# Up-projections of a two-layer encoder: three couples of column groups per layer, and a finished group's convolution work issued after the next group's first weight splits

## The chip, the cores and the metric

The kernel runs on one core of one Trainium2 chip. The time is device microseconds of one execution. The kernel before takes 2450.95 us, the median of three runs (2449.8 to 2451.17). The profile is of one further execution, which took 2449.38 us; its profiled span is 2447.3 us, so 2.08 us of that time lie around the span.

Engines are named as in the profile: PE is TensorE (matmuls), PEld its weight loads, DVE is VectorE, ACT is ScalarE, POOL is GpSimd, SP is SyncE. SP and POOL here mostly issue transfers.

## The reference, cut to what matters

Two layers, 256 positions, width 2048, everything in float32. Each layer has a token mixer (a gated MLP with a spatial gate, then a latent attention) and after it the sub-layer that the change touches, a gated MLP with a causal depthwise convolution of width 3 between the up-projection and the activation:

```python
D_MODEL = 2048
SEQ = 256
D_FF = 5504
CONV_W = 3

def conv_ffn(x, w_up, conv_w, conv_b, w_down):
    h = x @ w_up                                   # 256 x 2048 by 2048 x 11008
    h = lax.conv_general_dilated(h, conv_w[:, None, :], window_strides=(1,),
                                 padding=[(CONV_W - 1, 0)],
                                 dimension_numbers=('NWC', 'WIO', 'NWC'),
                                 feature_group_count=C) + conv_b
    a, g = jnp.split(h, 2, axis=-1)
    return (jax.nn.silu(g) * a) @ w_down
```

Around it stand a residual sum and a layer norm: `x = layer_norm(ALPHA * x + f, g, b)`.

## The kernel before, in words

**Exactness by splitting.** A float32 weight tile `raw` is split on the chip into two halves in a faster matmul format: ACT casts it to `wh` (line 134) and DVE subtracts to get `wl` (line 137). Activations are split the same way and kept as `xhl`. A product is then the sum of three: high by high, low by high, high by low.

**The up-projection's groups.** The 11008 columns of `w_up` are worked in 22 groups (0 to 21) of 512 columns; a group's weights come as four chunks of 1 MB, each one SP transfer into one of three `raw` buffers. `feed.next()` hands out the next chunk and first issues the loads and splits of the two chunks behind it. A group is worked in one of two ways.

- A *plain* group (`plain`, `prod_a`) has columns on the partitions: the weights are the stationary operand and `xhl` streams past. Per chunk 16 matmuls of 512 streamed columns (`wh`) and 16 of 256 (`wl`), so 128 matmuls per group into four of the eight PSUM banks.
- A *couple* of groups (`summed`) has tokens on the partitions: the weights stream past stationary pieces of `xhl`. Its eight chunks are taken in the order `UP_PAIRS`. Four of them go through `eight` (24 matmuls of 512 columns), the four in `UP_SEVEN` through `seven`, a seven-product scheme for a 2x2 block product (21 matmuls of 512). It needs sums of activations (`sums`, made once per layer by `combine_up`, tiles `xu`) and sums of weights (`ts`, line 144, and their split halves `th`, `tl`), and all eight banks, named q3, p2, e, q4, p1, q5, p7, p6. Afterwards DVE folds the banks together (`rest`, lines 475 to 478, and four final sums), and PE turns the four results back to columns on the partitions with 16 transposes of 128x128 (`turn_back`, line 1049), which stand after the first chunk of the following plain group.

**After a group.** `pair` makes one 128-row tile of the activation from two accumulators: ACT copies half a bank (`lo`, line 409), DVE adds the other half (`h`, line 411), then the convolution takes one ACT pass (line 1023) and two DVE passes (lines 1024, 1026), then SiLU on ACT (line 1040) and a product on DVE (line 1041). A plain group has two pairs; they run while the next group is on PE. The two `h` reads of a pair are what frees a bank for the next owner. After a couple there are four pairs, called by the plain group behind it (`both`), without the `lo` and `h` steps.

**Small work among the groups.** The table `EARLY` places, by group and chunk, the four `combine_up`, the residual's last scaling (`restore`, four DVE operations of 128x512 each and two row loads on the SP queue, lines 738 to 742) and the copying of the residual's two halves to memory (`park`, POOL queue, line 718). From group 10 on, `jobs` copies eight chunks of the down-projection's weights, split and summed in advance, out to memory (`park_all`: loads `praw`, casts `pwh`, `pth`, line 172, subtractions line 173, sums line 161, four stores per chunk, lines 166 and 189, all on the POOL queue); the calls are counted out by group and chunk.

**What sets the order.** The program's text gives priorities, and a scheduler orders each engine's queue from it with its own model of durations; what is marked `keep_in_program_order` stays as written. Every engine works its queue strictly in order. On-chip memory is handed out from pools: 14 tiles of 8 KB per partition in "big" (weight halves, `xhl`, the residual, most of the activation), 6 in "side", 3 `raw`.

Of the kernel before, what the change touches and what calls it, by code (L numbers as in the profile page):

```python
# [15 lines left out]
P = 128  # L16
# [53 lines left out]
LEAD = 5  # L70
KEEP = {"wide": 4, "seven": 6, "parked": 6}

UP = [(1,), (2,), (3,), (4,), (5, 6), (7,), (8, 9), *((i,) for i in range(10, 22))]
UP_PAIRS = [0, 2, 1, 3, 5, 4, 6, 7]
UP_SEVEN = (2, 3, 4, 6)
EARLY = {(1, 2): ("restore", 0), (2, 1): ("combine", 0), (2, 2): ("restore", 1), (2, 3): ("park", 0),
         (3, 1): ("restore", 2), (3, 2): ("combine", 1), (3, 3): ("restore", 3), (4, 0): ("park", 1),
         (4, 1): ("combine", 2), (4, 2): ("combine", 3)}


def plan(n_k):
# [140 lines left out]
def trunk(ctx: ExitStack, tc: tile.TileContext, x, xT, gm_in, gm_wout, ffn_up, ffn_dn,  # L222
# [807 lines left out]
    def ffn(layer, ln, acc, end, last):  # L1030
# [39 lines left out]
        def combine_up(p):  # L1070

            x = xhl[p // 2][:, p % 2 * 2 : p % 2 * 2 + 2]
            y = tp.tile([P, 2, S], F32, tag="t2", name=f"upy{layer}_{p}", bufs=T2)
            nc.vector.tensor_tensor(y, x[:, :, 0:S].bitcast(F32), x[:, :, S : 2 * S].bitcast(F32), ALU.add)
            if len(sums) % 2 == 0:
                rooms.append(slot([P, 2, 8 * P], f"xu{layer}_{p}", F32R))
            sums[p] = combine(f"u{layer}_{p}", rooms[-1][:, len(sums) % 2, :], y[:, 0], y[:, 1])

        early = {"restore": old.restore, "park": old.park, "combine": lambda i: combine_up(UP_SEVEN[i])}

        def plain(gi, turned):

            nt, nk = (4, 4) if gi < 21 else (2, 8)
            acc = [bank(f"up{layer}_{gi}_{f}") for f in range(nt)]
            for c in range(KD // nk):
                hi, lo = feed.next()
                prod_a(acc, xhl, range(nk * c, nk * c + nk), hi, lo)
                if c == 0 and turned:
                    for i, t in enumerate(turned[2]):
                        turn_back(turned[1][i % 2], t, i // 2)  # L1090
                if turned and 0 < c < 3:
                    both(turned[0][c - 1], turned[1][c - 1])
                if (gi > 9 and c > 0) or (gi, c) == (7, 3):
                    next(jobs, None)
                if (gi, c) in FIRST:
                    acts.make(*plan(NF_FF)[0][FIRST.index((gi, c))])
                if gi == 1 and c == 0:
                    after(1, 1, None)
                    both(0, hb)
                if (gi, c) in EARLY:  # L1100
                    name, i = EARLY[gi, c]
                    early[name](i)
            for f in range(nt // 2):
                pair(2 * gi + f, acc[f], acc[nt // 2 + f])

        def summed(gis):

            acc = Banks(f"up{layer}_{gis[0]}", DIRECT + OWN)
            for p in UP_PAIRS:
                a = [[x_parts(xhl, 2 * p + j, b) for j in range(2)] for b in range(2)]  # L1110
                got = feed.next()
                if p in UP_SEVEN:
                    acc.seven(a, sums[p], *got, turned=512, across=True)
                    if p == UP_SEVEN[-1]:
                        rest = acc.rest()
                else:
                    acc.eight(a, *got, across=True)
            for n, t in zip(DIRECT, rest):
                nc.vector.tensor_tensor(t, acc.acc[n], t, ALU.add)
            return gis, [[bank(f"upr{layer}_{gi}_{f}") for f in range(2)] for gi in gis], rest  # L1120
# [440 lines left out]
```

## Time and profile before

| what | value |
|---|---|
| median of three runs | 2450.95 us (2449.8 to 2451.17) |
| the profiled execution | 2449.38 us, span 2447.3 us |
| PE busy | 2440.4 us, 100% of the span |
| DVE busy | 2191.0 us, 90% |
| ACT busy | 1512.4 us, 62% |
| POOL busy | 140.6 us, 6% |
| granted TensorE clock | 1.00 |
| mean memory traffic | 256 GB/s |

The busy share of PE says that it is never long without work; how fast that work goes is read from the starts of its matmuls, since their ends are modelled. The up-projection's plain groups and couples follow each other on PE without other work between them: in layer 0 groups 1 to 4, then the couple of 5 and 6, group 7, the couple of 8 and 9, and groups 10 to 21. Layer 1 repeats this about 955 us later.

### The profile page before, as it was taken

To read this page: it belongs to the slowest core of one execution; us is meant where nothing else is said; L and a number is where in the kernel's file an instruction comes from. 1 tells how busy PE (TensorE), PEld (TensorE's weight loads), DVE (VectorE), ACT (ScalarE), POOL (GpSimd) and SP (SyncE) were. 2 spreads that over 40 slices of the span, in tenths; PEclk is the share of its full clock that TensorE was granted. 3 is DMA by queue.
4 is the path that set the end of the run, shared out by engine and by line. 5 is a ranking of instruction groups with operands and counts; after the bars stand their busy time and mean duration, and the time that the engine had idled before them with its cause. 6 is when DMAs were issued, how large, how long until landed. Compare 5 with 4: busy or idle time off the path is not lost.

```text
span 2447.3 us, 32249 instructions
## 1 busy us (share of the span) xinstructions
PE 2440.4 (100%) x12151; PEld 2065.3 (84%) x12151; DVE 2191.0 (90%) x2914; ACT 1512.4 (62%) x1997; POOL 140.6 (6%) x261
## 2 busy tenths in 40 slices
PE   9999999999999999999999999999999999999999
PEld 7888888888888888888888888988888888888887
DVE  7999999899998889998889897878798999888998
ACT  6666665566576655666665566665655666666553
POOL 0000000001010000011000000000000001010000
PEclk9999999999999999999999999999999999999999
DMA  7555666658796755799988885533575589898894
GB/s 293 203 205 205 233 202 205 207 173 304 254 296 241 239 205 194 258 359 374 341 318 320 320 298 172 188 141 126 207 272 184 181 323 375 321 371 300 314 353 178
DMA packets 128763, 627.37 MB, mean 256 GB/s; under 512 B 11592, under 2 KB 15184, under 8 KB 91616
## 3 DMA queue, kind: packets, MB, share of 16 engines
q1 hardware_dynamic: 94224, 462.47, 53.5%
q0 software_dynamic: 34384, 162.86, 17.9%
q8 instruction: 95, 1.56, 0.3%
q14 instruction: 60, 0.49, 0.1%
HBM read 552.35 MB, written 72.93 MB: 256 GB/s over the span
## 4 chain that ended last, share of the span: by engine, by line
PE 97%; DVE 1%; DMA 1%; ACT 0%; issue 0%; POOL 0%; ACTq 0%; DVEq 0%; POOLq 0%
PE up L242 30%; PE ub L242 16%; PE dn_q L242 8%; PE dn_p L242 6%; PE v_q L242 5%; PE v_p L242 4%; PE up_q L242 3%; PE up_p L242 3%; PE wo_q L242 2%; PE dn_e L242 2%; PE wo_p L242 2%; PE upf L242 2%; PE mo L242 2%; PE v_e L242 2%; PE mkv L242 1%; PE qn L242 1%
## 5 line engine op out<-in xcount | busy, mean ns | idle before, releaser
L137 DVE TENSOR_TENSOR wl<-raw,wh 128x1024 fp32r<-128x1024 f32 (+5 forms) x611 | 936.3, 1550 | 108.9 <-ACT wh L134 77.4
L134 ACT CAST wh<-raw 128x1024 fp32r<-128x1024 f32 (+5 forms) x611 | 790.9, 1318 | 307.2 <-PE up L242 67.8
L242 PE MATMUL up<-xhl,wh 128*128 128x512 f32 x2112 | 492.9, 390 | 0.0
L242 PEld LDWEIGHTS up<-xhl,wh 128*128 128x128 f32 x2112 | 392.3, 188 | 78.7
L134 ACT CAST th<-ts 128x1536 fp32r<-128x1536 f32 x196 | 203.7, 1051 | 173.9 <-DVE ts L144 144.2
L242 PEld LDWEIGHTS up<-xhl,wl 128*128 128x128 f32 x2112 | 262.4, 192 | 5.1
L242 PE MATMUL up<-xhl,wl 128*128 128x256 f32 x2112 | 265.1, 283 | 0.0
L137 DVE TENSOR_TENSOR tl<-ts,th 128x1536 fp32r<-128x1536 f32 x196 | 231.6, 1219 | 7.9 <-ACT th L134 3.3
L242 PE MATMUL ub<-wh,xhl 128*128 128x512 f32 x552 | 172.0, 393 | 0.0
L144 DVE TENSOR_TENSOR ts<-ts,raw 128x512 f32<-128x512 f32 x196 | 134.7, 687 | 2.0
L242 PEld LDWEIGHTS ub<-wh,xhl 128*128 128x128 f32 x552 | 103.6, 188 | 23.2 <-issue 1.9
L144 DVE TENSOR_TENSOR ts<-raw 128x1024 f32<-128x1024 f32 x98 | 119.5, 1219 | 2.2 <-DMA raw<-in_gm_in_dram 0.8
L242 PE MATMUL ub<-wl,xhl 128*128 128x512 f32 x276 | 107.5, 389 | 0.0
L242 PE MATMUL v_q<-wh,xhl 128*128 128x512 f32 x224 | 70.8, 391 | 0.0
L242 PEld LDWEIGHTS ub<-wl,xhl 128*128 128x128 f32 x276 | 51.8, 188 | 10.9
L242 PE MATMUL v_p<-wh,xhl 128*128 128x512 f32 x192 | 59.9, 389 | 0.0
L242 PEld LDWEIGHTS v_q<-wh,xhl 128*128 128x128 f32 x224 | 42.1, 188 | 9.7 <-ACT wh L134 0.9
L832 ACT ACTIVATE lny<-lnt,lncol 128x128 f32<-128x128 f32 x96 | 36.6, 471 | 15.7 <-PE lnt L828 15.6
L161 DVE TENSOR_TENSOR praw<-praw 128x512 f32<-128x512 f32 x64 | 43.9, 686 | 0.5
L242 PE MATMUL v_q<-wl,xhl 128*128 128x512 f32 x112 | 43.6, 389 | 0.0
L242 PE MATMUL mo<-wh,oT 128*128 128x512 f32 x128 | 42.7, 411 | 0.0
L242 PEld LDWEIGHTS v_p<-wh,xhl 128*128 128x128 f32 x192 | 36.0, 188 | 7.5
(2073 smaller groups left out, 4824.9 us busy)
## 6 DMA issues: line engine op xcount, KB each, us to landing
raw<-in_ffn_up_dram SPq DMA_DIRECT2D x172, 1024.0 KB, 5.9
raw<-in_gm_in_dram SPq DMA_DIRECT2D x93, 1024.0 KB, 5.3
raw<-in_ffn_dn_dram SPq DMA_DIRECT2D x68, 1024.0 KB, 7.7
raw<-in_gm_wout_dram SPq DMA_DIRECT2D x48, 1024.0 KB, 6.4
praw<-in_ffn_dn_dram POOLq DMA_DIRECT2D x16, 1024.0 KB, 12.5
keptth<-pth POOLq DMA_DIRECT2D x16, 1024.0 KB, 8.5
kepttl<-ptl POOLq DMA_DIRECT2D x16, 1024.0 KB, 8.7
fth<-keptth POOLq DMA_DIRECT2D x16, 1024.0 KB, 9.5
```

The source lines that it names most:

```text
L134: cast = self.nc.scalar.copy(hi, raw)
L137: self.nc.vector.tensor_tensor(lo, raw, hi.bitcast(F32), ALU.subtract)
L144: add = lambda o, a, b: self.nc.vector.tensor_tensor(o, a, b, ALU.add)
L161: add = lambda o, a, b: pin(nc.vector.tensor_tensor(o, a, b, ALU.add))
L242: recent[0] = nc.tensor.matmul(o, l, r, start=start, stop=stop, skip_group_check=True)
L832: nc.scalar.activation(y[:, j], t[:, j * P : (j + 1) * P], AF.Identity, bias=lncol[:, o : o + 1], scale=lncol[:, g : g + 1])
```

## The change

The table `UP` of a layer goes from two couples, (5, 6) and (8, 9), to three, (3, 4), (6, 7) and (9, 10). So groups 3, 4 and 10 are no longer plain, groups 5 and 8 are, and from group 1 on 15 groups are plain where 17 were (the last, group 21, is half a group).

With it: the four `combine_up` move into groups 1 and 2, since the first couple needs them there; the activation sums go to the "side" pool; the second half of the residual is scaled and copied out late (written at groups 12, 16 and 17); the calls of `jobs` begin one group later and come four to a group, not three, in groups 13 to 15. And a plain group no longer calls `pair` at its end: it puts its two pairs on a list, and the next group's first chunk calls them (`settle`) after `feed.next()`, that is, after the splits which that call issues. From group 19 on the list is emptied at the group's end as before.

```diff
-UP = [(1,), (2,), (3,), (4,), (5, 6), (7,), (8, 9), *((i,) for i in range(10, 22))]
+UP = [(1,), (2,), (3, 4), (5,), (6, 7), (8,), (9, 10), *((i,) for i in range(11, 22))]
-EARLY = {(1, 2): ("restore", 0), (2, 1): ("combine", 0), (2, 2): ("restore", 1), (2, 3): ("park", 0),
-         (3, 1): ("restore", 2), (3, 2): ("combine", 1), (3, 3): ("restore", 3), (4, 0): ("park", 1),
-         (4, 1): ("combine", 2), (4, 2): ("combine", 3)}
+EARLY = {(1, 1): ("restore", 0), (1, 2): ("combine", 0), (1, 3): ("combine", 1), (2, 0): ("restore", 1),
+         (2, 1): ("combine", 2), (2, 2): ("park", 0), (2, 3): ("combine", 3),
+         (12, 0): ("restore", 2), (16, 0): ("restore", 3), (17, 0): ("park", 1)}
...
-                rooms.append(slot([P, 2, 8 * P], f"xu{layer}_{p}", F32R))
+                rooms.append(slot([P, 2, 8 * P], f"xu{layer}_{p}", F32R, "side"))
...
+        waiting = []
+
+        def settle():
+
+            while waiting:
+                pair(*waiting.pop(0))
...
                 hi, lo = feed.next()
+                settle()
                 prod_a(acc, xhl, range(nk * c, nk * c + nk), hi, lo)
...
-                if (gi > 9 and c > 0) or (gi, c) == (7, 3):
+                if (gi > 10 and (c > 0 or 12 < gi < 16)) or (gi, c) == (8, 3):
                     next(jobs, None)
...
-            for f in range(nt // 2):
-                pair(2 * gi + f, acc[f], acc[nt // 2 + f])
+            waiting.extend((2 * gi + f, acc[f], acc[nt // 2 + f]) for f in range(nt // 2))
+            if gi > 18:
+                settle()
...
                 got = feed.next()
+                settle()
                 if p in UP_SEVEN:
```

The change as the scheduler lays it out, at three places. **PE, second chunk of the first couple of layer 0.** The names are banks and weight halves; `wh165` and `wh157` are the couple's second chunk, `wh166` and `wh158` its third. Before, with the couple of 5 and 6:

```order
L242 MATMUL up0_5_p1_7092<-wh165_7002,xhl1_1_5899 128x512 x2
L242 MATMUL up0_5_p1_7092<-wl165_7003,xhl1_1_5899 128x512
L242 MATMUL up0_5_q4_7091<-th165_7004,xhl1_1_5899 128x512 x2
L242 MATMUL up0_5_q4_7091<-tl165_7005,xhl1_1_5899 128x512
L242 MATMUL up0_5_q5_7093<-th165_7004,xu0_2_6495 128x512 x2
L242 MATMUL up0_5_q5_7093<-tl165_7005,xu0_2_6495 128x512
L242 MATMUL up0_5_p7_7094<-th165_7004,xu0_2_6495 128x512 x2
L242 MATMUL up0_5_p7_7094<-tl165_7005,xu0_2_6495 128x512
L242 MATMUL up0_5_p6_7095<-th165_7004,xu0_2_6495 128x512 x2
L242 MATMUL up0_5_p6_7095<-tl165_7005,xu0_2_6495 128x512
```

Now, with the couple of 3 and 4, the last products of the second chunk stand behind most of the third:

```order
L242 MATMUL up0_3_q4_6630<-wh158_6635,xhl1_0_5898 128x512 x2
L242 MATMUL up0_3_q4_6630<-wl158_6636,xhl1_0_5898 128x512
L242 MATMUL up0_3_p7_6633<-th157_6573,xu0_2_6333 128x512 x2
L242 MATMUL up0_3_p7_6633<-tl157_6574,xu0_2_6333 128x512
L242 MATMUL up0_3_q4_6630<-wh158_6635,xhl1_0_5898 128x512 x2
L242 MATMUL up0_3_q4_6630<-wl158_6636,xhl1_0_5898 128x512
L242 MATMUL up0_3_q3_6627<-wh159_6704,xu0_2_6333 128x512 x2
L242 MATMUL up0_3_q3_6627<-wl159_6705,xu0_2_6333 128x512
L242 MATMUL up0_3_p2_6628<-wh159_6704,xhl1_1_5899 128x512 x2
L242 MATMUL up0_3_p6_6634<-th157_6573,xu0_2_6333 128x512 x2
L242 MATMUL up0_3_p6_6634<-tl157_6574,xu0_2_6333 128x512
```

Counted in the couple's matmuls, p7 was first written after 39 of them and is now after 60, p6 after 42 and now after 71; p1 stays at 30, and q5 goes from 36 to 39. In the couples of 6 and 7 and of 9 and 10 p7 comes after 58 and 42, p6 after 65 and 61; before, in the couple of 8 and 9, after 48 and 59.

**DVE at the start of that couple.** `h` rows read the last plain group's banks and free them; `wl` of the couple's third chunk is `wl166` before and `wl158` now. Before:

```order
L411 TENSOR_TENSOR h_0a8_7052<-up0_4_0_6858,lo_0a8_7050 128x256
L1024 SCALAR_TENSOR_TENSOR c_0a8_7054<-h_0a8_7052,cst_176,c_0a8_7054 128x255
L411 TENSOR_TENSOR h_0g8_7060<-up0_4_2_6860,lo_0g8_7058 128x256
L1026 SCALAR_TENSOR_TENSOR c_0a8_7054<-h_0a8_7052,cst_176,c_0a8_7054 128x254
L1024 SCALAR_TENSOR_TENSOR c_0g8_7062<-h_0g8_7060,cst_176,c_0g8_7062 128x255
L1026 SCALAR_TENSOR_TENSOR c_0g8_7062<-h_0g8_7060,cst_176,c_0g8_7062 128x254
L1041 TENSOR_TENSOR act0_1_7049<-s0_8_7066,c_0a8_7054 128x256
L411 TENSOR_TENSOR h_0a9_7071<-up0_4_1_6859,lo_0a9_7069 128x256
L137 TENSOR_TENSOR wl166_7097<-raw166_6958,wh166_7096 128x2048
L1024 SCALAR_TENSOR_TENSOR c_0a9_7073<-h_0a9_7071,cst_176,c_0a9_7073 128x255
L411 TENSOR_TENSOR h_0g9_7079<-up0_4_3_6861,lo_0g9_7077 128x256
```

Now:

```order
L137 TENSOR_TENSOR wl158_6636<-raw158_6534,wh158_6635 128x2048
L316 TENSOR_TENSOR xsu0_6_6620<-xsu0_6_6620,upy0_6_6618 128x128
L411 TENSOR_TENSOR h_0a4_6643<-up0_2_0_6390,lo_0a4_6641 128x256
L317 TENSOR_TENSOR xsu0_6_6620<-upy0_6_6618,xsu0_6_6620 128x128
L144 TENSOR_TENSOR ts159_6703<-raw159_6584 128x1024
L326 TENSOR_TENSOR xu0_4_6522<-xsu0_6_6620,xu0_4_6522 128x512
L1024 SCALAR_TENSOR_TENSOR c_0a4_6645<-h_0a4_6643,cst_176,c_0a4_6645 128x255
L411 TENSOR_TENSOR h_0g4_6651<-up0_2_2_6392,lo_0g4_6649 128x256
L1026 SCALAR_TENSOR_TENSOR c_0a4_6645<-h_0a4_6643,cst_176,c_0a4_6645 128x254
L144 TENSOR_TENSOR ts159_6703<-ts159_6703,raw159_6584 128x512
L1024 SCALAR_TENSOR_TENSOR c_0g4_6653<-h_0g4_6651,cst_176,c_0g4_6653 128x255
L137 TENSOR_TENSOR wl159_6705<-raw159_6584,wh159_6704 128x1536
```

The third chunk's `wl` went from behind three of the four bank reads to ahead of all of them, and the fourth chunk's sums and split stand among them. The two remaining bank reads, `h_0a5` and `h_0g5`, follow 4 and 7 rows after the last row shown, with `ts159`, `act0_0` and the first piece of `tl159` between.

**SP, where the second half of the residual's rows are loaded.** Before, among the loads of groups 3 and 4:

```order
L738 DMA lnp0_20_6715<-in_ln_rows_dram 128x512
L738 DMA lnp0_21_6717<-in_ln_rows_dram 128x512
L109 DMA raw158_6509<-in_ffn_up_dram 128x2048
L109 DMA raw159_6557<-in_ffn_up_dram 128x2048
L109 DMA raw160_6641<-in_ffn_up_dram 128x2048
L738 DMA lnp0_30_6812<-in_ln_rows_dram 128x512
L738 DMA lnp0_31_6814<-in_ln_rows_dram 128x512
```

Now, among the loads of group 12 (chunks 192 to 195):

```order
L738 DMA lnp0_20_8397<-in_ln_rows_dram 128x512
L109 DMA raw192_8079<-in_ffn_up_dram 128x2048
L738 DMA lnp0_21_8399<-in_ln_rows_dram 128x512
L738 DMA lnp0_30_9294<-in_ln_rows_dram 128x512
L109 DMA raw193_8135<-in_ffn_up_dram 128x2048
L738 DMA lnp0_31_9296<-in_ln_rows_dram 128x512
L109 DMA raw194_8205<-in_ffn_up_dram 128x2048
```

All four row loads moved behind the last couple; the scheduler did not leave those of the fourth quarter at group 16, where the text has them. The POOL queue's copy of the residual's second half (line 718) moved with them, from ahead of the first `praw` to behind the third.

## The prediction

> **What bounds the kernel now.** I read the page first, then the chain of waits in order of time, then the stages one by one, then the waits and the timelines inside a couple.
>
> ```profile
> span 2447.3 us, 32249 instructions
> PE 2440.4 (100%) x12151; PEld 2065.3 (84%) x12151; DVE 2191.0 (90%) x2914; ACT 1512.4 (62%) x1997; POOL 140.6 (6%) x261
> PE 97%; DVE 1%; DMA 1%; ACT 0%; issue 0%; POOL 0%; ACTq 0%; DVEq 0%; POOLq 0%
> ```
>
> PE is the bound: 97% of the chain is its own. A change gains what it takes out of PE's stream and loses what it makes PE wait for. VectorE at 90% comes next. The chain through layer 0's up-projection (start, length, matmuls; the last row from the whole span's chain):
>
> ```profile
> 816.36 83.36 PE up L242 x480
> 899.72 1.36 PE up_q L242 x6
> 940.52 5.54 PE up L242 x32
> 946.06 1.75 PE upr L1049 x16
> 964.49 1.36 PE up_q L242 x6
> 1005.64 5.54 PE up L242 x32
> 1012.93 250.06 PE up L242 x1440
> ```
>
> The plain lengths count to the next row's start, so they are rates and not modelled ends. A plain group of 128 matmuls takes 83.36 / 480 x 128 = 22.23 us, and 250.06 / 1440 gives the same: the plain groups run without a gap. The first couple lasts from 899.72 to 940.52, 40.80 us for 180 matmuls, 226.7 ns each; its 16 transposes take 1.75 us in the next group. The second lasts 1005.64 - 964.49 = 41.15 us, 0.35 more for the same work. What was late there, and how near VectorE is, say the waits of this stretch and the stages (length, PE, weight loads, VectorE, ScalarE, POOL; clock, DMA share, GB/s):
>
> ```profile
> PEld up_q L242 <- DVE tl L137: 0.4, 1, 0.4
> PEld up_p L242 <- DVE h_0a L411: 0.2, 1, 0.2
> 899.72:940.52 40.80, 40.80 (x181) 33.78 (x181) 37.04 (x43) 25.38 (x28) 0.00 (x0) 1.00 0.53 185
> 940.52:964.49 23.97, 23.97 (x145) 21.43 (x145) 22.41 (x36) 14.13 (x21) 0.00 (x0) 1.00 0.59 195
> 964.49:1005.64 41.15, 41.15 (x181) 33.61 (x181) 38.82 (x44) 24.70 (x27) 0.00 (x0) 1.00 0.55 191
> 1096.30:1140.80 44.50, 44.50 (x257) 39.39 (x257) 40.39 (x56) 28.56 (x40) 5.19 (x9) 1.00 1.00 387
> ```
>
> A couple leaves VectorE 2 to 4 us. There PE already waits for it, for a split and for a bank read, if only by tenths.
>
> **The change, part by part.** *A couple for two plain groups.* Two plain groups cost 2 x 22.23 = 44.46 us, a couple 40.80 + 1.75 = 42.55: 1.91 us less in each layer, **3.82 us** in both. This is PE's own stream, so the gain is in the end time unless a wait eats it.
>
> *VectorE in a couple.* Prices from the first couple's timeline, where it works without a break. What counts is the step to the next start, a little less than the printed length (second column); the last two rows are of group 3:
>
> ```profile
> 905.69 2.29 DVE L137 TENSOR_TENSOR wl<-raw,wh 128x2048 fp32r<-128x2048 f32 x1 [1.31 <-ACT wh L134]
> 907.90 0.48 DVE L1024 SCALAR_TENSOR_TENSOR c_0a<-h_0a,cst,c_0a 128x255 f32<-128x255 f32 x1
> 908.29 0.42 DVE L411 TENSOR_TENSOR h_0g<-up,lo_0g 128x256 f32<-128x256 f32 x1
> 908.63 0.47 DVE L1026 SCALAR_TENSOR_TENSOR c_0a<-h_0a,cst,c_0a 128x254 f32<-128x254 f32 x1
> 909.02 1.22 DVE L144 TENSOR_TENSOR ts<-raw 128x1024 f32<-128x1024 f32 x1
> 910.15 0.48 DVE L1024 SCALAR_TENSOR_TENSOR c_0g<-h_0g,cst,c_0g 128x255 f32<-128x255 f32 x1
> 910.55 0.68 DVE L144 TENSOR_TENSOR ts<-ts,raw 128x512 f32<-128x512 f32 x1
> 911.15 0.47 DVE L1026 SCALAR_TENSOR_TENSOR c_0g<-h_0g,cst,c_0g 128x254 f32<-128x254 f32 x1
> 911.54 1.75 DVE L137 TENSOR_TENSOR wl<-raw,wh 128x1536 fp32r<-128x1536 f32 x1
> 913.21 0.68 DVE L144 TENSOR_TENSOR ts<-ts,raw 128x512 f32<-128x512 f32 x1
> 913.82 0.42 DVE L1041 TENSOR_TENSOR act<-s,c_0a 128x256 f32<-128x256 f32 x1
> ...
> 859.10 0.28 DVE L314 TENSOR_TENSOR xsu<-upy 128x128 f32<-128x128 f32 x1
> 859.30 0.28 DVE L315 TENSOR_TENSOR xsu<-upy 128x128 f32<-128x128 f32 x1
> ```
>
> So 2.21 us for 2048 columns, 1.67 for 1536, 1.13 for 1024, 0.60 for 512, 0.20 for 128; 0.39 for a convolution pass, 0.34 for an `h` or an activation product. An eight-product chunk takes 2.21, a seven-product one 1.13 + 3 x 0.60 + 2 x 1.67 = 6.27, a pair 2 x (0.34 + 2 x 0.39) + 0.34 = 2.58. A couple asks 4 x (2.21 + 6.27) + 2 x 2.58 = 39.1 of its 40.80 us. The Trainium skill speaks against a third couple here: VectorE: DVE Perf Modes, "The DRAIN you can't avoid", has the next operation start only when the pipeline has emptied. By printed lengths the same work comes to about 42.7 us and every couple would lose 1.9; the steps above disagree, and so do the first couple's 40.80 us.
>
> *The first couple comes two groups earlier.* From group 1's start to the third chunk's `wl` of that couple VectorE now has six plain chunks (6 x 2.26 = 13.6), the two pairs of group 0 (3.8), two `restore` (8 x 0.60 = 4.8), group 1's pairs (5.2), most of four `combine_up` at 2 x 0.60 + 4 x 0.20 (7) and the couple's first two chunks (8.5): 43 us. In groups 1 and 2 before, it stood still for 4.4 and 1.1 us:
>
> ```profile
> 811.10:833.30 22.20, 22.20 (x131) 19.74 (x130) 17.84 (x26) 14.16 (x19) 0.00 (x0) 1.00 0.73 258
> 833.30:855.50 22.20, 22.20 (x129) 19.66 (x128) 21.15 (x36) 12.48 (x20) 0.55 (x1) 1.00 0.87 297
> ```
>
> With those 5.4 us again it is there after 48.4, 3.9 us after the couple's start at 44.5. The plain groups lose nothing: their splits are ahead by two chunks.
>
> *The deferred pairs.* This wait is new: the `h` reads that free the last plain group's four banks now stand behind the third chunk's split, with the fourth chunk's split among them, and PE is queued behind them in the second chunk's last products. ScalarE's share, from the first couple's timeline:
>
> ```profile
> 899.08 0.37 ACT L409 COPY lo_0a<-up 128x256 f32<-128x256 f32 x1 [2.72 <-PE up L242]
> 903.74 1.91 ACT L134 CAST wh<-raw 128x2048 fp32r<-128x2048 f32 x1
> 905.55 0.60 ACT L1023 ACTIVATE c_0a<-h_0a,cst 128x256 f32<-128x256 f32 x1
> 913.93 0.62 ACT L134 CAST th<-ts 128x512 fp32r<-128x512 f32 x1 [0.81 <-DVE ts L144]
> ```
>
> The first copy can end 0.3 us before the couple starts (899.45 against 899.72). Behind it stand a `th` of 512 (0.6) and the third chunk's `wh` (1.81), so the `wl` can begin 2.1 us after the start. From there to the end of the last read, `h_0g5`, VectorE has 2.21 + 2 x 1.67 + 1.13 + 3 x 0.60 + 5 x 0.39 + 5 x 0.34 + 2 x 0.20 = 12.5 us. The bank is free at 14.6 us, or at 16.4 with the backlog of 3.9; PE asks for it after 71 matmuls, at 71 x 0.2267 = 16.1. That is from 1.5 us to spare to 0.3 late. Behind groups 5 and 8 the same walk leaves under 1 us at several places, the nearest p7 of the third couple (42 matmuls, 9.5 us). An unseen wait, so bounds: nothing at all, or 0.35 us, the second couple's loss now, in each of three. I take 0.35 per layer in all, as now, by the row of that couple: **zero** net.
>
> *Moved small work.* Two `restore` (4.8 us of VectorE), four row loads on SP and one POOL copy go from groups 2 to 4 to groups 11 to 13, and the parked weights have nine groups where they had ten, one chunk in each of 13 to 15. VectorE then has 4 x 2.26 + 5.2 + (1.67 + 4 x 0.60 + 2.21) = 20.5 of 22.23 us there. On SP `raw193` and `raw194` stand behind row loads that want a small tile from the couple's transposes, some 7.3 us into group 11; their chunks are used 20 us later. Cost zero, hidden by the 11 us that splits run ahead; without that cover it is the second rival.
>
> **Sum.** 2449.38 - 3.82 = 2445.56 us for a profiled execution. The runs' median lies 1.57 above the profiled one, so **2447.1 us**, 0.16% less. A measurement of this kernel tells about 0.2%, 4.9 us, from no change, so the likeliest outcome is a gain just inside that.
>
> **The rivals.** *VectorE late in every couple* (the other side). Place: the bank reads at the couples' second chunk and the `tl` of the fourth. For it: 39.1 of 40.80 us, and both waits above. Against it: the second couple, behind a group in which VectorE was busy 22.41 of 23.97 us, lost only 0.35. Price: with printed lengths in place of steps 1.9 us in each of six couples, 11.4 less the 0.70 paid now: 2447.1 + 10.7 = **2457.8 us**. It decides from (3.82 + 0.70) / 6 = 0.75 us a couple upward.
>
> *Memory traffic in groups 13 to 15.* The stretch around groups 14 and 15 already shows a DMA share of 1.00 at 387 GB/s. Its transfers between groups 11 and 20 (GB/s in 40 slices; issue to landing in us last), and ScalarE's waits for weights:
>
> ```profile
> GB/s 358 351 390 342 401 419 424 426 422 245 231 307 311 420 408 411 333 417 410 310 415 394 269 396 339 375 164 265 309 262 415 337 349 388 426 419 393 238 253 404
> raw<-in_ffn_up_dram SPq DMA_DIRECT2D x37, 1024.0 KB, 8.8
> keptth<-pth POOLq DMA_DIRECT2D x8, 1024.0 KB, 8.6
> keptwh<-pwh POOLq DMA_DIRECT2D x7, 768.0 KB, 9.4
> ACT wh L134 <- DMA raw<-in_ffn_up_dram: 13.9, 7, 3.6
> ```
>
> A group with one parked chunk moves 4 + 1 + 2 x 1 + 2 x 0.75 = 8.5 chunks of 1.05 MB, 8.9 MB: 23.0 us at 387 GB/s, 20.9 at 426. At the lower rate 0.8 us in three groups of two layers, 4.7 us: **2451.8 us**. Against it: slices up to 426, and PE did not wait here. DMA: Bandwidth & Descriptors, "Queues, rings and completion order", in the Trainium skill, lets each engine take turns between queues by packets; then the stores, not the weights, would be late.
>
> *The old stall goes too.* The deferral puts `tl` ahead of the pairs' work, and the 0.35 us vanish with nothing new: 2447.1 - 0.7 = **2446.4 us**.
>
> **How the numbers follow.** The forecast gets 0.60, the vanished stall 0.18, late VectorE 0.13, traffic 0.09. Faster by over 0.2% means under 2446.05 us: half of the vanished stall's share and a tenth of the forecast's lie there by the scatter of the runs, together 0.16. Slower by over 0.2% is late VectorE down to 1.6 us a couple, 0.12. The rest, 0.72, is within. The range runs from 2445.7, below the clean case, to 2451.8, the traffic's; left out are most of late VectorE and some scatter, under 0.2.
>
> **What would show it.** Right: couples of 40.8 to 41.2 us each, three in a layer; plain groups at 22.23; groups 11 to 21 without a gap; no PE wait for `h` above 0.5 us. Wrong: PE waits for `h_0a`, `h_0g` or `tl` of a microsecond in every couple, VectorE busy throughout (first rival); or ScalarE's `wh` waiting for `raw` in groups 13 to 15 and gaps among the plain matmuls there (second); or stalls in the down-projection, which I take as untouched.

## The result: slower, by the stretch I had taken as covered

The changed kernel takes 2467.48 us (median of 6 runs, 2465.12 to 2468.74), the kernel before 2450.67 us beside it. The ratio is 1.0068, 95% interval 1.0057 to 1.0079: slower by 0.7%. I had forecast 2447.1 us, with a range of 2445.7 to 2451.8. The profiled execution took 2468.74 us, 19.4 more than the one before.

First the page of the changed kernel: span, engines and the shares of the chain of waits.

```profile
span 2467.0 us, 32069 instructions
PE 2443.6 (99%) x12031; PEld 2057.2 (83%) x12031; DVE 2221.9 (90%) x2938; ACT 1516.8 (61%) x1983; POOL 140.6 (6%) x261
PE 73%; issue 15%; DVE 6%; DMA 4%; ACT 1%; POOL 1%; SPq 0%; POOLq 0%; ACTq 0%; DVEq 0%
```

The chain was 97% PE; now it is 73%, with VectorE and transfers in it. That is the mark of a kernel that has left its bound. Where it happens, the stages tell (length, PE, weight loads, VectorE, ScalarE, POOL; clock, DMA share, GB/s): layer 0's three couples and its plain groups 11 to 21 from the end of the last couple's transposes on, the same stretch of layer 1, and for comparison the plain groups 10 to 21 before, which are one group more.

```profile
856.12:897.02 40.90, 40.90 (x181) 33.71 (x181) 39.72 (x49) 24.87 (x28) 0.00 (x0) 1.00 0.58 194
920.98:962.15 41.17, 41.16 (x182) 33.66 (x181) 39.97 (x46) 25.83 (x30) 0.00 (x0) 1.00 0.58 191
986.12:1027.56 41.44, 41.44 (x182) 33.57 (x181) 37.72 (x44) 24.76 (x28) 0.00 (x0) 1.00 0.51 171
1034.85:1274.24 239.39, 230.76 (x1314) 202.06 (x1314) 208.95 (x301) 149.29 (x207) 24.97 (x44) 1.00 0.92 352
2000.05:2237.31 237.26, 230.17 (x1315) 201.90 (x1314) 209.48 (x301) 149.46 (x208) 24.94 (x44) 1.00 0.93 356
...
1012.93:1262.99 250.06, 250.06 (x1441) 221.47 (x1441) 222.46 (x315) 162.24 (x226) 24.41 (x43) 1.00 0.92 349
```

The couples do what the sum asked of them: 40.90, 41.17 and 41.44 us. The plain stretch does not. Its 1312 matmuls at the rate before (250.06 / 1440 each) are 227.8 us; it takes 239.4 and, in layer 1, 237.3. So 11.6 + 9.4 = 21.0 us are lost there, and that is nearly the whole difference: -3.8 + 21.0 + 1.6 in both layers' couples = 18.8 of the 19.4 us. By the starts of the matmuls, groups 12 and 13 of layer 0, where the moved `restore` calls run, lose 2.0 of the 11.6 us, groups 16 and 17 lose 7.7 and group 20 loses 1.6.

What PE waits for in layer 0's stretch (us in total, times, longest; the three rows make 8.7 us, and the other 2.9 stand in the profile as PE's own time, 230.8 us and not 227.8):

```profile
PE up L242 <- DVE wl L137: 7.5, 7, 1.4
PE up L242 <- DVE h_0g L411: 0.8, 1, 0.8
PE up L242 <- DVE c_0a L1026: 0.4, 1, 0.4
```

VectorE's split is late, though over the stretch VectorE works 209.0 of 239.4 us, and by PE's own pace would have had 18.9 us to spare. A total with room in it and an engine that is late all the same: the room must be lost in waits. The chain of waits, in order of time, shows one round of it, in group 12:

```profile
1060.10 0.60 DVE sum L742
1060.70 1.14 DVE wl L137
1061.84 2.20 DVE ptl L173
1064.04 0.40 DVE c_0g L1024
1064.43 1.14 DVE wl L137
1065.64 10.61 DMA raw<-in_ffn_up_dram
1076.39 0.89 issue
1077.28 1.04 ACT wh L134
1078.32 0.33 ACT s L1040
```

A moved `restore` step (`sum L742`) and a parked chunk's `ptl` stand before the last half of a split; only that half frees one of the three `raw` tiles, and the load that waits for it starts at 1065.64 and lands 10.6 us later. ScalarE and VectorE show the other half of the round:

```profile
1076.33 1.99 ACT L134 CAST wh<-raw 128x1024 fp32r<-128x1024 f32 x2 [4.39 <-DMA raw<-in_ffn_up_dram]
1078.23 0.41 ACT L1040 ACTIVATE s<-c_0g 128x256 f32<-128x256 f32 x1
...
1078.67 0.42 DVE L1041 TENSOR_TENSOR act<-s,c_0a 128x256 f32<-128x256 f32 x1 [3.33 <-ACT s L1040]
```

ScalarE stands 4.39 us at the cast of that load; the activation `s` of an older group is queued behind the cast, and VectorE, which wants `s`, stands 3.33 us. So late VectorE makes a late load, a late load a late ScalarE, and that a later VectorE. In group 17, where most is lost, the load is a parked chunk's, issued behind the stores of the chunk before it:

```profile
1158.92 13.82 DMA praw<-in_ffn_dn_dram
...
1172.83 1.47 ACT L172 CAST pwh<-praw 128x1536 fp32r<-128x1536 f32 x1 [5.01 <-DMA praw<-in_ffn_dn_dram]
...
1174.84 0.48 DVE L1024 SCALAR_TENSOR_TENSOR c_0g<-h_0g,cst,c_0g 128x255 f32<-128x255 f32 x1 [4.41 <-ACT c_0g L1023]
```

ScalarE stands 5.01 us at the cast, and VectorE 4.41 us for a convolution pass (`c_0g`) queued on ScalarE behind it. What VectorE loses in such rounds is its lead: the time from the end of a half split to the first matmul that reads it. The traces of the experiments show below what became of it.

### The profile page after: what moved, and what is told of

Its sections match the earlier page's. It is cut to its first block, busy times and chain, and to the rows that moved or that the text cites. A ratio compares the mean times of both kernels' runs of the same rounds, so it can differ in the third digit from the quotient of the medians.

```text
span 2467.0 us, 32069 instructions
## 1 busy us (share of the span) xinstructions
PE 2443.6 (99%) x12031; PEld 2057.2 (83%) x12031; DVE 2221.9 (90%) x2938; ACT 1516.8 (61%) x1983; POOL 140.6 (6%) x261
## 4 chain that ended last, share of the span: by engine, by line
PE 73%; issue 15%; DVE 6%; DMA 4%; ACT 1%; POOL 1%; SPq 0%; POOLq 0%; ACTq 0%; DVEq 0%
PE ub L242 16%; PE up L242 9%; PE dn_q L242 7%; PE dn_p L242 6%; PE v_q L242 5%; PE v_p L242 4%; PE wo_q L242 2%; DVE wl L137 2%; PE up_q L242 2%; PE dn_e L242 2%; PE up_p L242 2%; PE wo_p L242 2%; PE upf L242 2%; PE mo L242 2%; PE v_e L242 2%
## 5 line engine op out<-in xcount | busy, mean ns | idle before, releaser
L137 DVE TENSOR_TENSOR wl<-raw,wh 128x1024 fp32r<-128x1024 f32 (+4 forms) x595 | 930.5, 1580 | 93.4 <-ACT wh L134 79.5
L134 ACT CAST wh<-raw 128x1024 fp32r<-128x1024 f32 (+4 forms) x595 | 785.4, 1342 | 272.6 <-DMA raw<-in_ffn_up_dram 79.6
L242 PE MATMUL up<-xhl,wh 128*128 128x512 f32 x1856 | 435.2, 390 | 3.6 <-DVE c_1a L1026 1.6
L242 PEld LDWEIGHTS up<-xhl,wh 128*128 128x128 f32 x1856 | 344.2, 188 | 74.7 <-issue 3.1
L137 DVE TENSOR_TENSOR tl<-ts,th 128x1536 fp32r<-128x1536 f32 x212 | 250.9, 1219 | 5.4 <-PE v_p L242 1.9
L242 PE MATMUL up<-xhl,wl 128*128 128x256 f32 x1856 | 237.2, 284 | 12.1 <-DVE wl L137 12.1
L242 PEld LDWEIGHTS up<-xhl,wl 128*128 128x128 f32 x1856 | 231.6, 191 | 19.5 <-DVE wl L137 14.8
L242 PE MATMUL up_q<-wh,xhl 128*128 128x512 f32 x192 | 59.8, 389 | 0.0
L242 PE MATMUL up_p<-wh,xhl 128*128 128x512 f32 x192 | 59.1, 389 | 0.0
L173 DVE TENSOR_TENSOR ptl<-praw,pth 128x2048 fp32r<-128x2048 f32 x16 | 36.6, 2290 | 9.0 <-ACT pth L172 9.0
## 6 DMA issues: line engine op xcount, KB each, us to landing
fth<-keptth POOLq DMA_DIRECT2D x16, 1024.0 KB, 10.3
```

The lines of the kernel that those rows point to most:

```text
L134: cast = self.nc.scalar.copy(hi, raw)
L137: self.nc.vector.tensor_tensor(lo, raw, hi.bitcast(F32), ALU.subtract)
L173: pin(nc.vector.tensor_tensor(lo[:, 0:cols], raw[:, o : o + cols], hi[:, 0:cols].bitcast(F32), ALU.subtract))
L242: recent[0] = nc.tensor.matmul(o, l, r, start=start, stop=stop, skip_group_check=True)
```

## The experiments

Every time is a median with its ratio to the kernel before on the same chip. The scheduler orders each engine's instructions anew for every kernel, so an edit can also move what it does not name; where that matters it is said.

**Undo one part of the change each.** `a_steps3`: parking at the density before, one group longer.

```diff
-                if (gi > 10 and (c > 0 or 12 < gi < 16)) or (gi, c) == (8, 3):
+                if (gi > 10 and c > 0) or (gi, c) == (8, 3):
```

> The changed kernel with three parking steps in each of groups 11 to 20, in place of four in groups 13 to 15; all else as changed. The changed kernel lost about 20 us against the clean sum, by gaps in the plain groups 11 to 20 (11.5 us of them in layer 0). Theory A (parking is too dense in groups 13 to 15: a parked chunk per group asks more of VectorE, ScalarE and the transfers than a group gives): most of the loss goes, 2448 to 2454 us. Theory B (the two restore calls moved into groups 12 and 16 make VectorE late): at most 2 us better, 2465 us. Theory C (the deferred pairs): no change, 2467 us. Theory D (the bytes are the bound: nine plain groups and not ten for the same parked bytes): some relief from spreading over one group more, 2457 to 2462 us.

2467.16 us, ratio 1.007 (1.0055 to 1.0085). The time is that of Theory C, but by accident, and no theory had this: the stretch itself is mended for the most part (229.2 us in layer 0), and the time is lost again behind it. Parking now ends in group 20, and in VectorE's order the last parked chunk's `ptl` stands ahead of a bank read that the down-projection waits for (VectorE, PE's waits, and the stage behind them):

```profile
1278.99 2.28 DVE L173 TENSOR_TENSOR ptl<-praw,pth 128x2048 fp32r<-128x2048 f32 x1
1281.19 0.41 DVE L411 TENSOR_TENSOR h_0a<-up,lo_0a 128x256 f32<-128x256 f32 x1
...
PE dn_p L242 <- DVE h_0a L411: 3.6, 2, 3.0
...
1282.40:1285.40 3.00, 3.00 (x8) 2.34 (x7) 3.00 (x8) 2.33 (x5) 0.00 (x0) 0.50 1.03 419
```

The last row has the clock after that wait at 0.50, of which more at the end.

`a_no_restore`: the two moved `restore` calls left out (part of the residual then lacks its scale and offset).

```diff
-         (12, 0): ("restore", 2), (16, 0): ("restore", 3), (17, 0): ("park", 1)}
+         (17, 0): ("park", 1)}
```

> The changed kernel without the restore calls of groups 12 and 16 (the scale and offset of two quarters of the residual are left out: 16 VectorE operations of 0.60 us and 8 row loads of 256 KB in both layers together). Theory B: VectorE gets 9.6 us back, and SP's weight loads no longer stand behind row loads that want a tile of the couple: at least 10 us of the 20 go, 2450 to 2457 us. Theory A: at most 3 us better, 2464 us or more. Theory C: no change. Theory D: 2 of 169 MB less, no more than 1 us better, 2466 us.

2446.97 us, ratio 0.9987 (0.9978 to 0.9997): the loss is gone, more wholly than Theory B said, and the time is my forecast's. Theory D falls: the same parked bytes in nine groups cost nothing. The run takes away more than work and row loads, though: without the calls the second half of the residual is copied out at 794.4 us and not at 1087.7, so its tile is free early too.

`a_pairs_end_late`: no deferral in the parking groups.

```diff
-            if gi > 18:
+            if gi > 10:
                 settle()
```

> The changed kernel with the pairs of groups 11 to 21 again at the group's end (the deferral stays for groups 1 to 10, where the couples are). Theory C (behind the next split the pairs free their banks and give their tiles back too late when VectorE runs without lead): most of the loss goes, 2448 to 2455 us. Theories A, B and D: no change, 2465 to 2470 us.

2456.92 us, ratio 1.0032 (1.0018 to 1.0045). Half of the loss goes. So the three parts are not alternatives; my reading is that each takes some of the same lead.

`a_three`: these three edits together.

> All three of these edits on the changed kernel at once: three parking steps per group, no restore calls in groups 12 and 16, the pairs of groups 11 to 21 at the group's end. Theories A, B, C: the loss in the plain groups is gone, 2446 to 2449 us, which is my forecast of 2447.1. Theory D (bytes in nine or ten groups): 4 us or more remain, 2451 us and above.

2459.03 us, ratio 1.0035 (1.0022 to 1.0048). The stretch is clean (227.92 us), and the wait at the head of the down-projection (3.0 us, `dn_p` for `h_0a`) is that of `a_steps3`. So parking has to end in group 19, as the denser parking of the changed kernel does.

**What in a `restore` call costs.** `a_rows_only` keeps the row loads and leaves the VectorE operations out; `a_ops_only` the other way round, on a resident tile.

```diff
+            if f > 1 and self.idx != 1:
+                return                                  # a_rows_only
...
+                row = [cst[:, 0:512], cst[:, 0:512]]    # a_ops_only, no row loads
```

> The changed kernel with the row loads of the restore calls in groups 12 and 16 kept on SP's queue and their 16 VectorE operations left out. Without both, 20.5 us were gone. Theory B1 (VectorE's own 4.8 us per layer are the cause): 2447 to 2450 us, as without both. Theory B2 (the row loads between the weight loads on SP's queue make the weights land late): 2460 us or more.

2451.01 us, ratio 1.0002 (0.9993 to 1.0012): the loads alone cost some 4 us (the residual's half is copied out at 794.4 us here too).

> The changed kernel with the 16 VectorE operations of the restore calls in groups 12 and 16 kept (on a tile that is resident, so their values are left out) and without the 8 row loads. Theory B1: 2462 to 2467 us, as changed. Theory B2: 2447 to 2450 us. If both the operations and the loads cost, both of these two runs lie in between.

2446.45 us, ratio 0.9986 (0.9977 to 0.9995). By its words this would be Theory B2, but its trace says otherwise: without rows to wait for, the scheduler put the operations before group 1 (802.9 to 808.1 us in layer 0). The run moved the work instead of keeping it, and tells nothing of the loads. What it does tell: there is room for the same work elsewhere.

`a_restore_pool`: the operations on POOL.

```diff
+            eng = nc.gpsimd if f > 1 and self.idx != 1 else nc.vector
-                nc.vector.tensor_tensor(self.r(b, f), self.r(b, f), row[0], ALU.mult)
+                eng.tensor_tensor(self.r(b, f), self.r(b, f), row[0], ALU.mult)
```

> The changed kernel with the operations of the restore calls in groups 12 and 16 on POOL in place of VectorE; the result is the same. Theory B1: VectorE has its 9.6 us back, 2447 to 2451 us, faster than before, unless POOL's operations hold up its own queue of parked chunks or VectorE beside it. Theory B2: 2463 us or more.

2482.93 us, ratio 1.0134 (1.0117 to 1.0151): the slowest of all runs, and no verdict on the two theories, since POOL held up VectorE. VectorE and POOL in layer 0:

```profile
1039.89 2.30 DVE L137 TENSOR_TENSOR wl<-raw,wh 128x1024 fp32r<-128x1024 f32 x1
1042.11 1.51 DVE L1042 TENSOR_TENSOR act<-s,c_0a 128x256 f32<-128x256 f32 x1
1054.52 1.23 DVE L137 TENSOR_TENSOR wl<-raw,wh 128x1024 fp32r<-128x1024 f32 x1 [5.97 <-DMA resd<-sum]
...
1039.81 3.52 POOL L743 TENSOR_TENSOR sum<-sum,lnp 128x512 f32<-128x512 f32 x2 [3.63 <-DMA lnp<-in_ln_rows_dram]
```

While POOL works, a half split takes 2.30 us and not 1.23, a product 1.51. And at 1054.52 VectorE stands 5.97 us for the store of the residual's second half (`resd`): the tile it wants to write is the one the residual takes. That store was the first hint at a second cause.

`b_restore_late`: the kernel before with only its third and fourth `restore` and the second `park` moved behind the couples.

```diff
-         (3, 1): ("restore", 2), (3, 2): ("combine", 1), (3, 3): ("restore", 3), (4, 0): ("park", 1),
+         (3, 2): ("combine", 1), (11, 0): ("restore", 2), (15, 0): ("restore", 3), (16, 0): ("park", 1),
```

> The kernel before with one part of the change alone: its third and fourth restore calls and the store of the second half of the residual go from groups 3 and 4 to groups 11, 15 and 16. Two couples and ten groups with parking, as before. If the restore calls are dear wherever the parked chunks are: 2458 us or more. If it takes both them and the denser parking in nine groups (VectorE stood still 27.6 of 250 us there before, which is room for 4.8): within 2 us of before, 2449 to 2452 us.

2451.78 us, ratio 1.0008 (0.9999 to 1.0017). In ten groups the same calls cost the plain stretch nothing (250.10 us), though the first couple took 41.49 us and not 40.80. The large loss takes something more of the change; that `a_steps3` has its stretch nearly whole speaks for the denser parking.

**Mend it, and take the other parts alone.** `a_side_rows` loads the rows early, into a tile that is free then:

```diff
+        def early_rows(self):
+            self.rows23 = slot([P, 2, 1024], f"lnrw{self.idx}", tag="side")
+            for j in range(2):
+                src = ln_rows[2 * self.idx + j : 2 * self.idx + j + 1, 1024:2048]
+                nc.sync.dma_start(self.rows23[:, j, :], src.to_broadcast([P, 1024]))
...
+        ln.early_rows()
         boundary(ln, acc, end, f"upf{layer}_", after)
```

> The changed kernel with the rows of the third and fourth restore call loaded ahead of the boundary into one tile of 8 KB of their own; the same 16 VectorE operations then stand before group 1 in VectorE's order and no longer in groups 12 and 13. The result is the same. Theory B (rows and operations of the restore calls use up VectorE's lead where the parked chunks are dense): the loss of 17 us goes, 2446 to 2448 us, 0.15% faster than before. If the operations cost the same wherever they stand: 2460 us or more. If they make VectorE late in the first couple instead: 2449 to 2453 us.

2446.94 us, ratio 0.9987 (0.9978 to 0.9995): 0.13% faster than before, the same result, and the time I had forecast for the change. Its plain stretches, in both layers:

```profile
1034.42:1262.33 227.91, 227.91 (x1315) 201.82 (x1314) 206.67 (x293) 150.59 (x208) 24.36 (x43) 1.00 0.94 364
1986.67:2214.60 227.93, 227.93 (x1315) 201.85 (x1314) 204.22 (x291) 149.71 (x207) 24.36 (x43) 1.00 0.94 362
```

PE is busy throughout, with more bytes per us (364 against 352 GB/s) than the kernel that lost.

`a_pairs_end_all`: the changed kernel without any deferral (`settle()` at once behind every group).

> The changed kernel with all pairs at the group's end again, also before the couples (the whole deferral undone). By my prediction's walk the deferral moves the bank reads behind the third split of a couple and nets zero there: the couples stay within 0.5 us of 40.9, 41.2 and 41.4, and the whole time is that of the run with the pairs of groups 11 to 21 at the end, 2457 us. If the deferral is what lets the couples run: the first split of each couple stands behind two pairs (5.2 us of VectorE), each couple loses 1 us or more, 2462 us and above.

2463.16 us, ratio 1.005 (1.0037 to 1.0064). The time lies with the second case, but the reason given there is wrong: the couples took 40.93, 41.19 and 40.80 us, no worse. The difference to 2457 is in the plain stretches (234.6 and 238.9 us, against 232.2 and 233.3 in `a_pairs_end_late`). From group 11 on the two versions have the same text; what differs there is the scheduler's order. So where VectorE has lost its lead some 8 us can be order alone; below, only larger differences are read as the price of an edit.

`b_dense`: the kernel before with the parking of the change.

```diff
-                if (gi > 9 and c > 0) or (gi, c) == (7, 3):
+                if (gi > 10 and (c > 0 or 12 < gi < 16)) or (gi, c) == (7, 3):
```

> The kernel before with its parking in nine groups, 11 to 19, with four steps in each of 13 to 15, as in the changed kernel; the restore calls stay in groups 1 to 3. If the density alone is enough for the loss: gaps in groups 13 to 17 and 2455 us or more. If it takes the restore calls as well (without them the changed kernel ran without loss): 2449 to 2452 us.

2449.84 us, ratio 0.9998 (0.9989 to 1.0007). Density alone costs nothing. `b_defer`: the kernel before with the deferral alone (the diff's `waiting` and `settle`).

> The kernel before with the deferred pairs alone. My prediction put them at zero net: 2449 to 2451 us. If they clear the old stall of the second couple: 2449.2 us. If they take away VectorE's lead in groups 10 to 18 by themselves: 2454 us or more.

2450.69 us, ratio 1.0003 (0.9994 to 1.0012). Neither does the deferral, though the first couple takes 41.47 us in layer 0 instead of 40.80.

**The work or the tile.** `a_side_pinned` is `a_side_rows` with the operations held where the changed kernel ran them:

```diff
-         (12, 0): ("restore", 2), (16, 0): ("restore", 3), (17, 0): ("park", 1)}
+         (12, 0): ("restore", 2), (13, 1): ("restore", 3), (17, 0): ("park", 1)}
...
+                pin(nc.vector.tensor_tensor(self.r(b, f), self.r(b, f), row[0], ALU.mult))
```

> The version whose rows stand in a tile of their own, with the 16 restore operations held in program order in groups 12 and 13, where the changed kernel ran them; no row load stands between the weight loads there. If VectorE's operations in that stretch are the larger part of the loss (without them, but with the row loads, 16 of 20 us were gone): 2457 to 2465 us, with gaps in groups 12 to 17. If it takes the row loads on SP's queue and their small tiles as well: 2447 to 2451 us.

2479.3 us, ratio 1.0117 (1.0102 to 1.0133): it takes no row load on SP's queue there to lose 29 us, more than I had expected of either theory. But two things came back at once: the work and a held tile. The residual's second half can be stored, and its large tile freed, only after `restore`. The store in the kernel before, in the changed one and in `a_side_rows` (POOL's timelines):

```profile
874.17 0.56 POOL L718 DMA_DIRECT2D resd<-sum  x1 [25.75 <-DVE wl L137]
1087.72 0.56 POOL L718 DMA_DIRECT2D resd<-sum  x1 [15.58 <-DVE sum L742]
808.16 0.55 POOL L718 DMA_DIRECT2D resd<-sum  x1 [49.60 <-DVE sum L750]
```

So in the changed kernel one of 14 large tiles is taken through all three couples and into group 13.

`a_side_end`: `a_side_rows` without the deferral.

> The version whose rows stand in a tile of their own, with all pairs at the group's end as in the kernel before. In the changed kernel the deferral cost the couples 0.6 us per layer (41.44 us against 40.80 in the third). If the deferral is worth nothing where VectorE has its lead: 2445 to 2447 us. If it carries the stretch with the parked chunks: 2450 us or more, with gaps there.

2447.8 us, ratio 0.9993 (0.9984 to 1.0001), within 0.9 us of the version with it. Where VectorE has its lead the deferral is worth nothing that can be measured here.

`a_side_ops` brings the work back without the tile, `a_side_hold` the tile without the work.

```diff
+                if (gi, c) in ((12, 0), (13, 1)):                     # a_side_ops
+                    for j in range(4):
+                        t = tp.tile([P, 512], F32, tag="t2", name=f"extra{layer}_{gi}{j}", bufs=T2)
+                        tc.keep_in_program_order(nc.vector.tensor_tensor(t, cst[:, 0:512], cst[:, 0:512], ALU.mult))
...
-         (12, 0): ("restore", 2), (16, 0): ("restore", 3), (17, 0): ("park", 1)}   # a_side_hold
+         (12, 0): ("restore", 2), (12, 2): ("restore", 3), (13, 0): ("park", 1)}
...
+            store = nc.gpsimd.dma_start(d, self.res.pop(h))
+            if h and self.idx != 1:
+                tc.keep_in_program_order(store)
```

> The version whose rows stand in a tile of their own (2446.9 us, its restore operations before group 1, the second residual half stored there too), with eight extra VectorE operations of 512 columns per layer held in groups 12 and 13; what they compute goes unused. In the held version (2479 us) two things came back: 4.8 us of VectorE work there, and one of the 14 large tiles taken by the residual half until group 13. If VectorE's work is what counts: 2457 us or more. If it is the tile: 2446 to 2449 us.

2467.43 us, ratio 1.0071 (1.0056 to 1.0086).

> The same version with the store of the second residual half held in POOL's order until group 13, behind the second parked chunk's last store; its operations stay before group 1. The residual then takes one of the 14 large tiles through the three couples and into groups 11 to 13, as in the changed kernel, and nothing is added to VectorE. If the tile is what counts: 2457 us or more, with couples at 40.9, 41.2 and 41.4 us as in the changed kernel. If VectorE's work counts: 2446 to 2449 us.

2465.77 us, ratio 1.0068 (1.0051 to 1.0085). Both expectations were written as either-or, and either edit alone brings a loss of the changed kernel's size back. They do it in different ways. PE's waits in the plain stretch of `a_side_ops`, and then of `a_side_hold`, with ScalarE at the place of the latter's stall (all of layer 0):

```profile
PE up L242 <- DVE wl L137: 6.4, 6, 1.5
...
PE up L242 <- DVE h_0g L411: 3.1, 1, 3.1
PE up L242 <- DVE h_0a L411: 2.0, 1, 2.0
...
1162.65 1.47 ACT L172 CAST pwh<-praw 128x1536 fp32r<-128x1536 f32 x1 [3.24 <-DMA praw<-in_ffn_dn_dram]
1164.35 0.35 ACT L409 COPY lo_0a<-up 128x256 f32<-128x256 f32 x1
```

With the work, splits are late, as in the changed kernel, and the couples stay at 40.80, 40.91 and 40.93 us. The lead shows why. Its least value in each of groups 12 to 20 of layer 0, in us from the end of a half split to the first matmul that reads it:

| group | 12 | 13 | 14 | 15 | 16 | 17 | 18 | 19 | 20 |
|---|---|---|---|---|---|---|---|---|---|
| `a_side_rows` | 10.4 | 6.2 | 9.7 | 8.0 | 8.1 | 4.3 | 5.1 | 7.3 | 2.0 |
| `a_side_ops` | 10.3 | 3.6 | 2.8 | 0.9 | 0.1 | 0.1 | 1.0 | 3.6 | 0.1 |
| the changed kernel | 4.0 | 0.1 | 4.4 | 0.8 | 0.1 | 0.1 | 1.0 | 3.6 | 0.1 |

The eight operations of `a_side_ops` run at 1072.8 to 1075 and 1087 to 1090 us, in group 13. They are 4.8 us of work, and two groups later 7 us of lead are gone. PE stands where nothing is left: of the 9.5 us lost, 8.1 fall in groups 16 and 17 and 1.3 in group 20, much as in the changed kernel (some 1.7 us of it is 3.4 us at half clock, see the end). The scheduler's order behind the added operations differs too; that order without them was not tried.

With the tile, the couples are those of the changed kernel (40.89, 41.19, 41.38), the splits are in time (a least lead of 3.5 us up to group 19), and two bank reads are late in group 17, since the scheduler put them behind a parked chunk's cast that waits 3.24 us for its load. This run is less clean: it also fixes the store's place in POOL's queue, among a parked chunk's stores, where it lands after 11.3 us and a cast stands 3.8 us for it. In the changed kernel the store lands after 4.2 us and no instruction waits for it, and `b_restore_late` holds the tile about as long (its store stands at 1080.8 us) without loss in the plain stretch. So a held tile with a late store can bring a loss of this size; that it has a part in the changed kernel's plain stretch is not shown. The added work alone gives that loss, its place and its waits. A deeper ring of `raw` or `praw` tiles, which would test the rounds of waits by themselves, was not tried.

## Why the prediction was wrong

**A couple for two plain groups.** Right. 3.82 us were to come out of PE's stream; the version that keeps all else in cover shows 2446.94 against 2450.33 us, 3.4 less.

**VectorE in a couple.** Right: 39.1 us of work by steps fitted. The couples of the changed kernel lost 0.1, 0.4 and 0.6 us. By the rule that opens the Trainium skill's VectorE: DVE Perf Modes, "The DRAIN you can't avoid", each would have lost 1.9 us; the section adds that an operation which is not held starts earlier, and these couples agree with that (in my rows a printed length of 2.29 us took a step of 2.21).

**The first couple two groups earlier.** Right in its outcome: the backlog that I had put at 3.9 us cost 0.1 us there (40.90).

**The deferred pairs.** I took 0.35 us of stall per layer; it was 1.1 (0.10 + 0.37 + 0.64), 1.6 more in both layers. Part of it comes with the held tile: in `a_side_rows`, where it is free, the three couples of layer 0 stall 0.57 us together, and in `a_side_end`, without the deferral, no less (0.61). The rival that the old stall would vanish fell too: with the deferral alone the second couple took 41.19 us, as before.

**Moved small work.** This step failed, and with it the forecast. I wrote "Cost zero, hidden by the 11 us that splits run ahead". Four things were wrong in it.
- The 11 us are two of a group's four chunks (22.23 / 2); no row of mine showed that the splits always are so far ahead. In the kernel before the least lead was 5.8 us in groups 11 to 19 of layer 0 and 2.8 in group 20. In `a_side_rows`, which has the change's groups without the moved work there, it was 4.3 us in groups 12 to 19 and 2.0 in group 20. That does not hide 4.8 us.
- I compared 20.5 us of VectorE work with 22.23 us of group and called it cover. That is a sum over an engine that never waits. Here VectorE waits for ScalarE and ScalarE for loads, `raw` loads among them that VectorE itself releases, so that 4.8 us of added work lost 9.5 us in layer 0 of `a_side_ops`.
- The sum also left the moved work out of the groups it moves to. I wrote "from groups 2 to 4 to groups 11 to 13", and the fourth `restore` did run in group 13, at 1083 to 1087 us. With its 2.4 us my own prices make 22.9 us, more than the group has.
- I counted what the moved calls issue, not what they hold. "One POOL copy" was the release of a large tile, put off from 874 to 1088 us. It shows in the couples, with some 0.5 us in layer 0's three; more is not shown.

The second rival had the sign and about the stretch right: I had named the cover and said that without it that rival applies, at 2451.8 us. Its groups were not: 13 to 15 lose 1.6 us in layer 0, 16 and 17 lose 7.7. Its mechanism, bytes, was not either (`a_side_rows` moves the same parked bytes at 364 GB/s without a wait of PE), and its price was under a quarter of the loss. My own row, ScalarE's `wh` 13.9 us waiting for `raw` in the kernel before, pointed at the round of waits, and I read it as traffic. That a kernel of the change's design came out at 2446.94 us, beside my 2447.1, bears out the gain of the couples and not this step.

**The range.** It ended at the traffic rival because the unknown cost of the moved work had a bound from above of nothing at all in my list. It should have had one: 4.8 us of VectorE work on the path in each layer, 9.6 us, would have put 2457 into the range; even that is half of what came.

## What to carry to other kernels

Where several in-order engines feed one another through short rings of tiles, judge added work by the least lead at and behind its place, not by idle time in total: in `a_side_ops`, with VectorE at 92% of the time that PE needed (209.3 of 227.8 us), the lead was gone three groups behind the added work. When work is moved, ask as well what it holds until then, and put it into the sum of the groups where the scheduler will really run it. The cheapest mend was not to make the work smaller but to give it its inputs early: the same operations, some 240 us sooner (802 in place of 1044 us), were free.

## What was not expected of the hardware

After a longer stand, PE ran at half its clock for some microseconds. Layer 0 of `a_side_hold` around its stall (behind the length stand the five engines, then the granted clock):

```profile
1163.00:1169.00 6.00, 0.86 (x4) 0.31 (x2) 4.52 (x7) 4.55 (x8) 1.19 (x3) 0.92 1.01 426
1169.50:1174.30 4.80, 4.80 (x13) 3.74 (x12) 3.59 (x7) 1.42 (x4) 0.09 (x1) 0.50 1.01 425
1174.50:1190.00 15.50, 15.50 (x99) 14.09 (x98) 13.92 (x23) 10.68 (x15) 0.56 (x1) 0.99 0.63 227
```

Behind 6 us with four matmuls, the next 4.8 us ran at 0.50, with the starts of 512-column matmuls 0.427 us apart and not 0.227: 13 of them cost 2.6 us on top of the stall. The Trainium skill's TensorE: Matmul & The Clock Gate, "Part 1: The HAM clock gate", tells of this: half clock after an idle window of about 3.4 us, full clock after a busy one. These rows agree, but the pause need not be so long. In `a_side_ops` two steps between matmuls of 1.8 and 1.2 us, at 1156.2 and 1158.9, were enough for a clock of 0.50 from 1160.1 to 1163.4 us, while a step of 2.0 us in layer 1 of the changed kernel (at 2017.3) left its profiled execution at 1.00. In four of the changed kernel's six executions the mean clock was 0.998 or 0.999, so stalls like these can cost clock as well.

POOL beside VectorE was dearer than its own time: in `a_restore_pool` a half split took 2.30 us and not 1.23. SBUF — State Buffer, "SBUF: two separate sides", in the Trainium skill, has the two engines share a pair of ports that one of them takes for a whole instruction when VectorE has two inputs in SBUF; the rows fit that.
